# Low parts of every second weight block made by an adding transfer, in a decoder layer

## The chip, the cores and the metric

The kernel runs on one core of a Trainium2 chip. The time is in device microseconds (us) of one execution of the whole program. Engines are named as the profile names them: PE (TensorE matmul), PEld (its weight loads), DVE (VectorE), ACT (ScalarE), POOL (GpSimd), SP (SyncE, which only issues transfers here).

## The reference

One layer of a hybrid decoder, float32 in and out, 512 tokens of width 1024, 256 memory tokens:

```
x = x + 0.5 * swiglu(rms_norm(x), ffn1_gate, ffn1_up, ffn1_down)      # width 2816
z = rms_norm(x) @ w_in                                                # 7 groups of 512 columns
x = x + concat(hgrn2(z...), short_conv(z...)) @ w_out
q = rms_norm(x) @ w_q_mem;  k, v = split(rms_norm(mem) @ w_kv_mem)    # 4 heads of 256
x = x + softmax(q k^T / 16) v @ w_o_mem
x = x + 0.5 * swiglu(rms_norm(x), ffn2_gate, ffn2_up, ffn2_down)
out = rms_norm(x)
```

Some 26 million weights of float32 are read once.

## The kernel before

**Three products for one.** PE multiplies in float32r, which keeps fewer bits than float32. So each operand is split into a high part (the value rounded to float32r) and a low part (the value minus the high part, rounded), and a product a b is made as a_hi b_hi + a_hi b_lo + a_lo b_hi: `mm3`, lines 118 to 120, or three written-out matmuls in the stages w_i, w_v and w2d.

**Weight blocks.** Weights come in 202 blocks (called units in the code) of 128 partitions by 1024 elements (896 for two thirds of w1d). `weight_steps` numbers them by `n`, from 0, in the order in which the program asks for them, and gives each three tiles: `raw` (as loaded), `whi` and `wlo`. `load` (L105) issues the transfer from the queue of SP; `split` makes the high part on ACT (L109, a copy that rounds) and the low part on DVE (L110, raw minus high part). The blocks by stage:

| blocks | stage | PE work of a block |
|---|---|---|
| 0 to 43 | w1: first FFN, gate and up | 24 matmuls of 512 columns |
| 44 to 67 | w1d: first FFN, down | 21 or 24 of 512 |
| 68 to 95 | w_in and w_i: mixer inputs | 24 of 512 |
| 96 to 103 | w_out: mixer output | 24 of 512 |
| 104 to 111 | w_k: keys of the memory | 24 of 256 |
| 112 to 119 | w_q: queries | 24 of 512 |
| 120 to 127 | w_v: values of the memory | 12 of 512 |
| 128 to 135 | w_o: attention output | 24 of 512 |
| 136 to 179 | w2: second FFN, gate and up | 24 of 512 |
| 180 to 201 | w2d: second FFN, down | 24 of 512 (the last three by tokens) |

**Buffers.** `raw`, `whi` and `wlo` have three buffers each (`wpool`), given out in turn. Inside the two FFN stages blocks with n % 4 == 3 take a fourth pair of `whi` and `wlo` from the FFN's own pool instead (`extra`). So a block's split can start when PE has finished with the block three before it, or four before it in the FFN; its raw buffer is loaded anew when the split of the block three before has been made.

**Order.** The program is written with tile pools; a scheduler fixes each engine's order when the program is built, and puts in the waits. Each engine then runs its own list in order. POOL has little to do: three slices of the first loads (L105 with `queue=nc.gpsimd`), the power -0.5 of each norm (L151, L527), and some of the last norm (L752, L759).

The first three blocks are loaded and split in slices together with x (`first_tile`).

## Time and profile before

| | |
|---|---|
| time, median of 2 runs | 1131.24 us (1131.12 to 1131.37) |
| the profiled execution | 1130.89 us, span 1129.1 us |
| PE busy | 1119.5 us |
| DVE busy | 572.8 us |
| ACT busy | 391.1 us |
| POOL busy | 18.0 us |
| granted clock of PE | 0.999 |
| read from HBM | 109.09 MB |

The profile is of one execution. Busy times are the sums of an engine's instructions. In a row of the timeline stand the start and the length in us, engine, line, operation, tiles (written <- read), and in brackets how long the engine idled before and what ended that. In a row of groups stand the count, the busy time in us and the mean of one in ns, and the idle time before them. In a row of waits stand who waited for whom, us in total, how many times, and the longest. Rows of transfers give the count, KB each and the median us from issue to landing. In a row by stretches stand the engines' busy times in the order PE, PEld, DVE, ACT, POOL, then the granted clock, the DMA engines' mean busy share and GB/s.

### The profile page before, as it was taken

The page shows a single profiled execution, that of the slowest core. Times are in us where ns is not written, and L with a number is a line of the kernel's source. Part 1 is how long each engine was busy: PE and PEld are TensorE (multiplying, and loading weights), DVE is VectorE, ACT ScalarE, POOL GpSimd, SP SyncE. Part 2 cuts the span into 40 slices and gives each one's busy share as a digit, 9 for nine tenths or more (in the row PEclk, how much of TensorE's full clock was granted, in tenths as well). Part 3 has the DMA queues.
Part 4 walks back from the last instruction along what each step waited for, and adds up shares of the span by engine and source line. Part 5 has one row for each costly group of instructions (what it writes and reads, how often), then busy time and mean ns, then how long its engine had stood idle before and what let it go on. Part 6 is the DMA issues. An engine that isn't in the chain of part 4 may idle for free. (4 is left out here: it accounts for less than half of the span.)

```text
span 1129.1 us, 12928 instructions
## 1 busy us (share of the span) xinstructions
PE 1119.5 (99%) x5232; PEld 937.8 (83%) x5232; DVE 572.8 (51%) x829; ACT 391.1 (35%) x542; POOL 18.0 (2%) x21
## 2 busy tenths in 40 slices
PE   9999999999999999999999999999999999999997
PEld 7888888888888888888889888888888888888886
DVE  7644444443333466885677556564544444432223
ACT  6422332222222344324455246342333222231123
POOL 0000000000000000000100000000000000000002
PEclk9999999999999999999999999999999999999999
DMA  6322332323333222222144323123232223323311
GB/s 227 129 99 98 102 94 94 96 87 98 103 96 100 75 96 82 85 75 87 63 131 134 121 82 131 57 94 123 92 103 94 94 94 98 107 93 99 106 57 75
DMA packets 33195, 112.02 MB, mean 99 GB/s; under 512 B 3968, under 2 KB 4736, under 8 KB 33136
## 3 DMA queue, kind: packets, MB, share of 16 engines
q1 hardware_dynamic: 30960, 108.02, 29.1%
q10 hardware_dynamic: 2016, 2.66, 0.7%
q8 instruction: 41, 0.67, 0.2%
q0 software_dynamic: 160, 0.52, 0.2%
q14 instruction: 18, 0.15, 0.0%
HBM read 109.09 MB, written 2.10 MB: 98 GB/s over the span
## 5 line engine op out<-in xcount | busy, mean ns | idle before, releaser
L109 ACT ACTIVATE whi<-raw 128x1024 fp32r<-128x1024 f32 (+4 forms) x208 | 213.0, 1027 | 624.4 <-PE ps_f L119 274.1
L110 DVE TENSOR_TENSOR wlo<-raw,whi 128x1024 fp32r<-128x1024 f32 (+4 forms) x208 | 245.4, 1182 | 190.9 <-ACT whi L109 190.6
L212 DVE TENSOR_TENSOR u_f<-ps_f,rsb_f 128x512 f32<-128x512 f32 x44 | 30.4, 690 | 125.5 <-PE ps_f L120 125.5
L209 DVE TENSOR_TENSOR t_f<-ps_f,rsb_f 128x512 f32<-128x512 f32 x44 | 30.4, 690 | 79.0 <-PE ps_f L120 79.0
L213 DVE TENSOR_TENSOR u_f<-u_f,t_f 128x512 f32<-128x512 f32 x44 | 30.3, 692 | 4.0
L210 ACT ACTIVATE t_f<-t_f 128x512 f32<-128x512 f32 x44 | 27.7, 630 | 1.6 <-DVE t_f L209 1.1
L118 PE MATMUL psk<-memh,whi 128*128 128x256 f32 x64 | 18.2, 285 | 0.0
L119 PE MATMUL psk<-meml,whi 128*128 128x256 f32 x64 | 18.1, 284 | 0.0
L120 PE MATMUL psk<-memh,wlo 128*128 128x256 f32 x64 | 18.1, 283 | 0.0
L120 PE MATMUL ps_f<-x_f10h,wlo 128*128 128x512 f32 x44 | 17.3, 392 | 0.6 <-DVE wlo L110 0.6
L118 PE MATMUL ps_f<-x_f11h,whi 128*128 128x512 f32 x44 | 17.3, 393 | 0.4 <-ACT whi L109 0.4
L119 PE MATMUL ps_f<-x_f12l,whi 128*128 128x512 f32 x44 | 17.3, 393 | 0.0
L118 PE MATMUL ps_f<-x_f20h,whi 128*128 128x512 f32 x44 | 17.2, 391 | 0.0
L118 PE MATMUL ps_f<-x_f21h,whi 128*128 128x512 f32 x44 | 17.2, 390 | 0.0
L118 PE MATMUL ps_f<-x_f12h,whi 128*128 128x512 f32 x44 | 17.2, 390 | 0.0
L120 PE MATMUL ps_f<-x_f20h,wlo 128*128 128x512 f32 x44 | 17.2, 390 | 0.0
L119 PE MATMUL ps_f<-x_f10l,whi 128*128 128x512 f32 x44 | 17.2, 390 | 0.0
L120 PE MATMUL ps_f<-x_f11h,wlo 128*128 128x512 f32 x44 | 17.2, 390 | 0.0
L120 PE MATMUL ps_f<-x_f12h,wlo 128*128 128x512 f32 x44 | 17.2, 390 | 0.0
L120 PE MATMUL ps_f<-x_f17h,wlo 128*128 128x512 f32 x44 | 17.2, 390 | 0.0
L120 PE MATMUL ps_f<-x_f27h,wlo 128*128 128x512 f32 x44 | 17.2, 390 | 0.0
L118 PE MATMUL ps_f<-x_f15h,whi 128*128 128x512 f32 x44 | 17.2, 390 | 0.0
(1021 smaller groups left out, 3054.8 us busy)
## 6 DMA issues: line engine op xcount, KB each, us to landing
raw<-in_w SPq DMA_DIRECT2D x85, 512.0 KB, 3.4
raw<-in_w_in SPq DMA_DIRECT2D x24, 512.0 KB, 3.4
raw<-in_w2d SPq DMA_DIRECT2D x22, 512.0 KB, 3.4
raw<-in_w1d SPq DMA_DIRECT2D x16, 448.0 KB, 3.3
raw<-in_w1d SPq DMA_DIRECT2D x8, 512.0 KB, 3.5
raw<-in_w_out SPq DMA_DIRECT2D x8, 512.0 KB, 3.5
raw<-in_w_k SPq DMA_DIRECT2D x8, 512.0 KB, 3.4
raw<-in_w_q SPq DMA_DIRECT2D x8, 512.0 KB, 3.5
```

Source lines behind the costliest of these rows:

```text
L109: nc.scalar.activation(hi[:, c], raw[:, c], AF.Copy)
L110: nc.vector.tensor_tensor(lo[:, c], raw[:, c], r32(hi[:, c]), ALU.subtract)
L118: nc.tensor.matmul(out, lhsT=wh, rhs=xh, start=first, stop=False)
L119: nc.tensor.matmul(out, lhsT=wh, rhs=xl, start=False, stop=False)
L120: nc.tensor.matmul(out, lhsT=wl, rhs=xh, start=False, stop=last)
L209: nc.vector.tensor_tensor(t, ps[0], bc, ALU.mult)
L210: nc.scalar.activation(t, t, AF.Silu)
L212: nc.vector.tensor_tensor(u, ps[1], bc, ALU.mult)
L213: nc.vector.tensor_tensor(u, u, t, ALU.mult)
```

## The change

From block 5 on, the low part of each odd block is made without DVE. ACT writes minus the rounded raw block into `wlo`, and a transfer on POOL's queue then adds the block, read once more from HBM, onto that. Even blocks, and blocks 0 to 3, are as before. Lines from 115 on stand five lines lower in the changed kernel; its subtraction for the other blocks is L115.

```
         def split(k0, k1):
             c = slice(k0 * b, k1 * b)
             nc.scalar.activation(hi[:, c], raw[:, c], AF.Copy)
-            nc.vector.tensor_tensor(lo[:, c], raw[:, c], r32(hi[:, c]), ALU.subtract)
+            if n % 2 and n > 3:
+
+                nc.scalar.activation(lo[:, c], raw[:, c], AF.Copy, scale=-1.0)
+                nc.gpsimd.dma_start(lo[:, c], src[:, c], accum_op=ALU.add)
+            else:
+                nc.vector.tensor_tensor(lo[:, c], raw[:, c], r32(hi[:, c]), ALU.subtract)
```

PE's order stays as it was, but for one matmul of the first norm. On ACT in the stage w_k, here from block 109 to 111 (`kh` is the high part of the finished keys, `rsb_xa` a norm's row; the last number of a name is the program's own), there stood before:

```order
L109 ACTIVATE whi109_4530<-raw109_4529 128x1024
L581 ACTIVATE kh_3944<-km2_4450 128x256
L109 ACTIVATE whi110_4565<-raw110_4564 128x1024
L581 ACTIVATE kh_3944<-km3_4485 128x256
L170 ACTIVATE rsb_xa_4492<-psb_xa_4489 128x512
L109 ACTIVATE whi111_4600<-raw111_4599 128x1024
L581 ACTIVATE kh_3944<-km4_4525 128x256
```

and there stand now:

```order
L109 ACTIVATE whi109_4582<-raw109_4581 128x1024
L112 ACTIVATE wlo109_4583<-raw109_4581 128x1024
L586 ACTIVATE kh_3990<-km2_4501 128x256
L109 ACTIVATE whi110_4618<-raw110_4617 128x1024
L586 ACTIVATE kh_3990<-km3_4537 128x256
L175 ACTIVATE rsb_xa_4544<-psb_xa_4541 128x512
L109 ACTIVATE whi111_4653<-raw111_4652 128x1024
L586 ACTIVATE kh_3990<-km4_4577 128x256
L112 ACTIVATE wlo111_4654<-raw111_4652 128x1024
```

The negatives (L112) have come in: block 109's right behind its high part, block 111's with a key's high part between. Block 107's stands like block 111's, with `kh` of `km0` between. On ACT in the stage w_v (blocks 123 to 127) there stood only the high parts, one behind the other; now:

```order
L112 ACTIVATE wlo123_5273<-raw123_5271 128x1024
L109 ACTIVATE whi123_5272<-raw123_5271 128x1024
L109 ACTIVATE whi124_5291<-raw124_5290 128x1024
L112 ACTIVATE wlo125_5310<-raw125_5308 128x1024
L109 ACTIVATE whi125_5309<-raw125_5308 128x1024
L109 ACTIVATE whi126_5328<-raw126_5327 128x1024
L112 ACTIVATE wlo127_5347<-raw127_5345 128x1024
L109 ACTIVATE whi127_5346<-raw127_5345 128x1024
```

Here, and through w2d, the negative goes ahead of the high part of its block. In w_out the negative of block 101 stands behind its high part and six other operations (`x_xa2h` and `sq_xa` belong to the next norm of x, `memh` and `sq_mem` to the memory):

```order
L109 ACTIVATE whi101_4244<-raw101_4243 128x1024
L129 ACTIVATE x_xa2h_4133<-xall_102,vec_97 128x512
L140 ACTIVATE sq_xa_4137<-xall_102 128x512
L140 ACTIVATE sq_mem_4144<-mem4_4140 128x256
L129 ACTIVATE memh_3992<-mem6_4192,vec_97 128x256 x2
L140 ACTIVATE sq_mem_4149<-mem4_4140 128x256
L112 ACTIVATE wlo101_4245<-raw101_4243 128x1024
```

Before, nothing of block 101 stood on ACT after its high part.

On POOL, whose list held only the norms' powers between the opening and the end, the transfers (L113) now stand between them, here from w_out to w_k:

```order
L113 DMA wlo103_4339<-in_w_out 128x1024
L156 TENSOR_TENSOR rst_mem_4288<-rs_mem_4286,mhalf_77 128x2
L113 DMA wlo105_4419<-in_w_k 128x1024
L113 DMA wlo107_4507<-in_w_k 128x1024
L156 TENSOR_TENSOR rst_xa_4460<-rs_xa_4458,mhalf_77 128x4
L113 DMA wlo109_4583<-in_w_k 128x1024
```

Each transfer waits for the negative that ACT writes, and the power behind it in the list waits for its issue.

## The prediction

> **What bounds the kernel now.** I read the page first, then the waits of the matmul engine, then the weight split's own lines, then the times at which single blocks are made and used.

> ```profile
> PE 1119.5 (99%) x5232; PEld 937.8 (83%) x5232; DVE 572.8 (51%) x829; ACT 391.1 (35%) x542; POOL 18.0 (2%) x21
> ```
> ```profile
> PE warm L71 <- DVE mhalf L61: 1.1, 1, 1.1
> PE ps_f L120 <- DVE wlo L110: 0.6, 1, 0.6
> PE ps_f L118 <- ACT whi L109: 0.4, 1, 0.4
> PE psw L118 <- ACT yh1h L539: 0.3, 1, 0.3
> ```

> PE is busy for 1119.5 of 1129.1 us, and everything it waits for adds up to 2.4 us. So nothing that DVE, ACT or POOL stop doing can give back more than those few us: the change can only hide, or cost. The question is whether each low part is still there when PE's first L120 matmul asks for it.

> ```profile
> L110 DVE TENSOR_TENSOR wlo<-raw,whi 128x1024 fp32r<-128x1024 f32 x183 | 223.7, 1223 | 144.2 <-ACT whi L109 144.1
> L109 ACT ACTIVATE whi<-raw 128x1024 fp32r<-128x1024 f32 x183 | 193.9, 1061 | 567.9 <-PE ps_f L119 268.2 <-PE pso L730 74.4 <-issue 68.5
> ```

> A full block costs ACT 1.06 us (high part) and DVE 1.22 us (low part). ACT's waits are for PE: it starts block n as soon as PE has let go of the buffers of block n-3 (n-4 in the FFN stages, where a fourth pair exists). What matters is therefore the time from that start to PE's first use of the low part. In the first FFN, block 33:

> ```profile
> 173.23 1.06 ACT L109 ACTIVATE whi<-raw 128x1024 fp32r<-128x1024 f32 x1 [3.84 <-PE ps_f L119]
> ```
> ```profile
> 189.98 0.39 PE L120 MATMUL ps_f<-x_f10h,wlo 128*128 128x512 f32 x1
> ```

> 16.75 us lie between. The same distance recurs through both FFN products, which hold most of the blocks.

> **The change, part by part.** 99 blocks (odd, from 5 to 201) lose the DVE subtraction: 99 x 1.22 = 121 us of an engine that PE does not wait for; worth nothing. They gain an ACT copy with scale -1, priced as the L109 copy of the same shape: 99 x 1.06 = 105 us on an engine at 35%, hidden in the long stretches by ACT's own 567.9 us of waiting. And they gain a transfer that POOL issues after that copy. The new chain for an odd block is: buffer free, high part and negative copy on ACT (in either order), POOL's issue, landing. Call the last two L.

> No accumulating transfer stands in the trace. The nearest rows are the plain loads (KB each, us from issue to landing):

> ```profile
> q1 hardware_dynamic: 30960, 108.02, 29.1%
> ...
> raw<-in_w SPq DMA_DIRECT2D x85, 512.0 KB, 3.4
> ...
> raw<-in_w POOLq DMA_DIRECT2D x1, 320.0 KB, 7.1
> ...
> raw<-in_w SPq DMA_DIRECT2D x1, 64.0 KB, 3.1
> raw<-in_w POOLq DMA_DIRECT2D x1, 64.0 KB, 4.9
> raw<-in_w ACTq DMA_DIRECT2D x1, 64.0 KB, 3.3
> ```

> A 512 KB load from SP lands in 3.4 us. POOL's 64 KB took 4.9 us where SP's and ACT's took 3.1 and 3.3: 1.7 us more for the queue. Queue 1 held 16 engines for 29.1% of 1129.1 us, 328.6 us for 108.02 MB, or 1.6 us for 0.524 MB; an addition must fetch the destination too, so I count this stream once more. **L = 3.4 + 1.7 + 1.6 = 6.7 us**, an estimate. Its lower end is the plain load, 3.4. Its upper end takes POOL's opening rows, where all queues were loaded: (7.1 - 4.9) / 256 KB = 8.6 ns per KB, so 4.9 + 448 x 8.6 ns = 8.8 for 512 KB, and 3.9 for the second stream: 12.6. I take 6.7 because most of the loads meet emptier queues than the opening.

> In the FFN, two ACT operations (0.96 us from start to start, 1.06 for the last) leave 16.75 - 2.02 = 14.7 us for L: hidden up to 12.6. The tight places are where a block's matmuls are short. First w_k (blocks 104 to 111, 256 columns), odd blocks 107, 109 and 111; ACT rows, then PE's first use of each low part:

> ```profile
> 601.57 1.06 ACT L109 ACTIVATE whi<-raw 128x1024 fp32r<-128x1024 f32 x1 [0.77 <-PE psk L119]
> 602.53 0.40 ACT L581 ACTIVATE kh<-km 128x256 fp32r<-128x256 f32 x1
> ...
> 608.26 1.06 ACT L109 ACTIVATE whi<-raw 128x1024 fp32r<-128x1024 f32 x1 [2.40 <-issue]
> ...
> 614.47 1.06 ACT L109 ACTIVATE whi<-raw 128x1024 fp32r<-128x1024 f32 x1 [1.48 <-PE psk L119]
> 615.43 0.40 ACT L581 ACTIVATE kh<-km 128x256 fp32r<-128x256 f32 x1
> ```
> ```profile
> 608.37 0.28 PE L120 MATMUL psk<-memh,wlo 128*128 128x256 f32 x1
> ...
> 614.58 0.28 PE L120 MATMUL psk<-memh,wlo 128*128 128x256 f32 x1
> ...
> 620.34 0.28 PE L120 MATMUL psk<-memh,wlo 128*128 128x256 f32 x1
> ```

> For 107 and 111 a kh copy stands between the high part and the negative. The negative ends at 602.53 + 0.40 + 1.06 = 603.99, at 608.26 + 0.96 + 1.06 = 610.28 and at 615.43 + 0.40 + 1.06 = 616.89, which leaves 4.38, 4.30 and 3.45 us. A stall moves everything behind it, but a block's buffer comes from three blocks back. So 107 stalls by L - 4.38; 109, whose buffer came free before that stall, only by the 0.08 that is left; 111, freed by block 108, moved with the first stall and stalls by L - 3.53. Together 2L - 7.83 = **5.6 us**.

> w_v (blocks 120 to 127, 12 matmuls each) puts the negative first. Blocks 123 and 127:

> ```profile
> 682.77 1.06 ACT L109 ACTIVATE whi<-raw 128x1024 fp32r<-128x1024 f32 x1 [0.36 <-PE psvm L645]
> ...
> 693.65 1.06 ACT L109 ACTIVATE whi<-raw 128x1024 fp32r<-128x1024 f32 x1 [1.66 <-PE psvm L645]
> ```
> ```profile
> 688.24 0.39 PE L644 MATMUL psvm<-wlo,memh 128*128 128x512 f32 x1
> ```
> ```profile
> 699.12 0.39 PE L644 MATMUL psvm<-wlo,memh 128*128 128x512 f32 x1
> ```

> 688.24 - 683.83 = 4.41 for 123, and the same for 127; 125 between them is covered by the first stall. 2 x (L - 4.41) = **4.6 us**. Three single blocks remain: 101 in w_out, whose negative now stands behind the last sq_mem; the last block, 201; and 131 in w_o, as an example of the next tightest.

> ```profile
> 575.40 0.40 ACT L135 ACTIVATE sq_mem<-mem 128x256 f32<-128x256 f32 x1
> ```
> ```profile
> 582.05 0.39 PE L120 MATMUL psw<-yc0h,wlo 128*128 128x512 f32 x1
> ```
> ```profile
> 1100.27 1.06 ACT L109 ACTIVATE whi<-raw 128x1024 fp32r<-128x1024 f32 x1 [4.38 <-PE pso L730]
> ```
> ```profile
> 1107.09 0.39 PE L729 MATMUL pso<-wlo,a_f221h 128*128 128x512 f32 x1
> ```
> ```profile
> 719.67 1.06 ACT L109 ACTIVATE whi<-raw 128x1024 fp32r<-128x1024 f32 x1 [4.62 <-PE pswo L119]
> ```
> ```profile
> 731.03 0.39 PE L120 MATMUL pswo<-at0h,wlo 128*128 128x512 f32 x1
> ```

> 101: 582.05 - (575.40 + 0.40 + 1.06) = 5.19, a stall of **1.5 us**. 201 (negative first): 1107.09 - 1101.33 = 5.76, a stall of **0.9 us** right before the end. 131: 731.03 - 721.69 = 9.34, hidden. Sum: 6L - 27.6 = 12.6 us, 1.1%.

> The rest costs nothing. The negative waits, as DVE's subtraction did, for PE's last low-part matmul of the buffer's former block; behind it on ACT stand the next high part and, in the FFN, the silu and the split of the product, and each is 1.06 us later at most, which the margin of 14.7 covers. On POOL the transfers share a queue with the six power operations of the norms; the closest is rst_xa, between the transfers of 107 and 109:

> ```profile
> 605.68 1.01 POOL L151 TENSOR_TENSOR rst_xa<-rs_xa,mhalf 128x4 f32<-128x4 f32 x1 [15.81 <-ACT whi L109]
> ```

> It runs after 107's negative (603.99) and is done before 109's (610.28). SP's reload of an odd block's raw buffer now waits for ACT's negative instead of DVE; raw blocks land well ahead. The engines' load in w_k, where a new transfer every 5.8 us meets two loads:

> ```profile
> 598.00:622.00 24.00, 24.00 (x199) 23.84 (x198) 17.45 (x29) 12.62 (x19) 1.01 (x1) 1.00 0.46 152
> ```

> A share of 0.46, with 3.2 us more per 5.8 us, comes to about full. That is why I do not go below 6.7 here.

> **The profiled execution** took 1130.89 us (span 1129.1), 0.35 below the median of 1131.24. 1130.89 + 12.6 = **1143.5 us**.

> **The rivals.** (a) *Hidden anyway, not slower than before.* If POOL's issue costs little and the addition nothing, L is near 4.4 and the sum is about 1 us (only 111): 1132. For it: the 3.4 us row. Against it: the 4.9 us row. It decides below L = 4.6. [...]

> (b) *The addition is slow: slower by over 2%.* If the engines add at half the pace at which they fetch the two streams (3.2 us more, L = 9.9), or the queues in w_k are full, L passes 8.4, where 6L - 27.6 is 22.6 us, 2% of 1131. At L = 10 the six tight stalls cost 32.4, and of the ten blocks with a margin like 131's (in w_in, w_q and w_o), whose stalls cover each other in pairs, five pay 0.7 each: 1167. At 12.6: 48.0 + 5 x 3.3, 1195. For it: no row shows an addition, and the opening's rows are slow. Against it: the FFN would still hide all of it.

> (c) *DVE holds up the issue.* If a transfer's issue waits for a DVE operation, it loses at most one of L110's 1.22 us: L = 7.9, sum 19.9, 1151. [...]

> (d) *It doesn't do what it says:* if the transfer wrote instead of adding, L would be 5.1 and the sum 3.8 us, 1135; inside the range.

> **How the numbers follow.** Forecast (L from 4.6 to 8.4, with (d)): 0.45. (a) 0.14. (b) 0.35, of which a third beyond L = 10.5. (c) 0.04. Faster by over 2%: PE's 1119.5 us forbid it, 0.02 for what I don't see. 2% is about what a measurement of this kernel tells from no change. So within 2%: 0.45 + 0.14 + 0.04 = 0.63; slower 0.35. The range runs from 1133 (half of (a) left out) to 1172 (L near 10.5).

> **What would show it.** The page: DVE down to about 450, ACT up to about 496, 99 rows of L113 transfers with about 6.7 us to landing. PE's waits: psk, psvm, psw and pso on wlo transfers of 2 to 3 us each, none for ps_f. If ps_f waits, L is over 14.7 and the time is far beyond my range. If PE waits at whi, ACT's added copies are late, which I costed at nothing. If L is right and the stalls are not at these blocks, my reading of the buffers is wrong.

## The result, and the profile after

| kernel | median us | profiled execution us | span us |
|---|---|---|---|
| before | 1131.24 | 1130.89 | 1129.1 |
| changed | 1160.91 (1159.06 and 1162.77) | 1159.06 | 1157.3 |

The ratio is 1.0264, 95% interval 1.0246 to 1.0282: slower by 29.7 us, where 12.6 were forecast. Between the two profiled executions lie 28.2 us.

The first part of the page (busy us and share of the span), and two of its queue lines (packets, MB, share of the 16 DMA engines' span):

```profile
PE 1126.5 (97%) x5232; PEld 940.7 (81%) x5232; DVE 463.2 (40%) x730; ACT 478.4 (41%) x641; POOL 104.1 (9%) x120
...
q1 hardware_dynamic: 30960, 108.02, 29.7%
q0 software_dynamic: 14416, 51.91, 25.0%
```

DVE fell to 463 us and the transfers stand on queue 0, as the change says. PE has the same 5232 matmuls, but is "busy" 7.0 us longer than in the 1119.5 us before: some matmuls became slower, not only later. PE's waits for transfers (us in total, times, longest):

```profile
PE psk L125 <- DMA wlo<-in_w_k: 5.9, 4, 2.1
PE psvm L649 <- DMA wlo<-in_w_v: 5.5, 2, 3.0
PE ps_f L125 <- DMA wlo<-in_w: 3.2, 1, 3.2
PE psw L125 <- DMA wlo<-in_w_out: 2.9, 1, 2.9
```

Eight waits for transfers, 17.5 us. By PE's rows they stand at blocks 101 (2.87), 105 (1.52), 107 (0.18), 109 (2.11), 111 (2.08), 123 (2.48), 127 (3.05) and 137 (3.17). Block 111, which the prediction worked out, now reads so; ACT's negative, then PE's first use of the low part:

```profile
624.13 1.04 ACT L112 ACTIVATE wlo<-raw 128x1024 fp32r<-128x1024 f32 x1
...
633.34 0.39 PE L125 MATMUL psk<-memh,wlo 128*128 128x256 f32 x1 [2.08 <-DMA wlo<-in_w_k]
```

From the negative's end (625.17) to the use lie 8.2 us. By stages, from POOL's issue to landing, beside SP's plain load of w_k (KB each, median us):

```profile
wlo<-in_w POOLq DMA_DIRECT2D x42, 512.0 KB, 7.5
...
wlo<-in_w2d POOLq DMA_DIRECT2D x11, 512.0 KB, 6.9
raw<-in_w_k SPq DMA_DIRECT2D x8, 512.0 KB, 4.1
...
wlo<-in_w_k POOLq DMA_DIRECT2D x4, 512.0 KB, 7.3
```

POOL issues 0.30 us after the negative's end; that comes on top.

Two more losses are not waits. The first is the clock granted to PE. Two pairs of neighbouring windows of 3.41 us, around the waits at 111 and at 123 (behind the five engines' times stands the granted clock; 1.00 is full):

```profile
630.77:634.18 3.41, 1.33 (x12) 1.13 (x11) 0.85 (x2) 2.31 (x3) 0.59 (x1) 1.00 0.59 175
634.18:637.60 3.42, 3.42 (x19) 3.42 (x18) 0.00 (x0) 0.00 (x0) 0.27 (x1) 0.50 0.87 199
...
702.45:705.86 3.41, 0.93 (x5) 0.47 (x4) 0.00 (x0) 2.00 (x2) 0.85 (x1) 1.00 1.03 324
705.86:709.28 3.42, 3.42 (x10) 2.65 (x9) 0.00 (x0) 0.00 (x0) 0.00 (x0) 0.50 1.05 259
```

PE was idle for 2.08 and 2.48 us in the first window of each pair, and ran the second one at half clock (1.00, then 0.50). There are three such windows, at 586.40, 634.18 and 705.86, behind the waits at 101, 111 and 123. PE had idled for 2.70 us in the window before the first of them (582.99 to 586.40). Each is recorded as 3.413 us long, and from the first to the second lie 14 times 3.413 us and to the third another 21 times: all three stand on one grid of such windows. In the first and the third a matmul of 512 columns started every 0.427 us, where 0.227 was usual in w_out and w_v. By the granted 0.50 each did the work of 1.7 us in 3.41, so they lost about 5.1 us together, as an estimate. Before the change there was no such window until PE had ended.

The second loss is at the end: POOL's last long operation of the program is a drain (three drains; shortest, median and longest in ns). Before and after:

```profile
L843 POOLq DRAIN  x3: 34/102/901, 1123.9 to 1128.7; - x3
```
```profile
L848 POOLq DRAIN  x3: 46/102/6782, 1149.7 to 1157.0; - x3
```

The long one takes 6.8 us in place of 0.9 and is over at 1156.48; SP's first drain, behind the outputs, stands at 1154.0 already. From PE's last matmul to the end of the span go 9.5 us in place of 7.1: 2.4 us.

**The account of the 28.2 us:** 17.5 of waits, 5.1 of half clock, 2.4 at the end, 1.3 at two small shifts (0.67 at block 4, 0.61 where PE waits for `yh1h`), and 1.4 behind the five waits that no half window follows (PE is 0.25 to 0.29 us later behind 105, 107, 109, 127 and 137 than the wait alone explains). 0.5 is left over. What makes the two small shifts, and the slower pace behind the five waits, is open.

### The profile page after: what moved, and what is told of

Its sections match the earlier page's. It is cut to its first block, busy times and chain, and to the rows that moved or that the text cites. A ratio compares the mean times of both kernels' runs of the same rounds, so it can differ in the third digit from the quotient of the medians.

```text
span 1157.3 us, 13129 instructions
## 1 busy us (share of the span) xinstructions
PE 1126.5 (97%) x5232; PEld 940.7 (81%) x5232; DVE 463.2 (40%) x730; ACT 478.4 (41%) x641; POOL 104.1 (9%) x120
## 3 DMA queue, kind: packets, MB, share of 16 engines
q1 hardware_dynamic: 30960, 108.02, 29.7%
## 5 line engine op out<-in xcount | busy, mean ns | idle before, releaser
L109 ACT ACTIVATE whi<-raw 128x1024 fp32r<-128x1024 f32 (+4 forms) x208 | 212.7, 1026 | 551.1 <-issue 226.3
L115 DVE TENSOR_TENSOR wlo<-raw,whi 128x1024 fp32r<-128x1024 f32 (+4 forms) x109 | 125.4, 1155 | 189.9 <-ACT whi L109 189.6
L112 ACT ACTIVATE wlo<-raw 128x1024 fp32r<-128x1024 f32 (+1 forms) x99 | 102.7, 1037 | 46.5 <-PE pso L734 37.3
L113 POOL DMA_DIRECT2D wlo<-in_w x42 | 36.0, 856 | 415.3 <-ACT wlo L112 415.3
L196 DVE SCALAR_TENSOR_TENSOR xall<-psd_f,xall 128x512 f32<-128x512 f32 x8 | 5.5, 692 | 41.7 <-PE psd_f L125 41.7
L113 POOL DMA_DIRECT2D wlo<-in_w_in x12 | 10.3, 857 | 128.9 <-ACT wlo L112 100.2
L113 POOL DMA_DIRECT2D wlo<-in_w1d x12 | 10.2, 852 | 111.3 <-ACT wlo L112 111.3
L113 POOL DMA_DIRECT2D wlo<-in_w2d x11 | 9.4, 853 | 112.9 <-ACT wlo L112 112.9
L649 PE MATMUL psvm<-wlo,memh 128*128 128x512 f32 x32 | 13.2, 412 | 5.5 <-DMA wlo<-in_w_v 5.5
L125 PEld LDWEIGHTS psk<-memh,wlo 128*128 128x128 f32 x64 | 12.9, 202 | 6.7 <-DMA wlo<-in_w_k 6.7
## 6 DMA issues: line engine op xcount, KB each, us to landing
raw<-in_w SPq DMA_DIRECT2D x85, 512.0 KB, 4.0
wlo<-in_w POOLq DMA_DIRECT2D x42, 512.0 KB, 7.5
raw<-in_w_in SPq DMA_DIRECT2D x24, 512.0 KB, 4.0
raw<-in_w2d SPq DMA_DIRECT2D x22, 512.0 KB, 4.2
wlo<-in_w_in POOLq DMA_DIRECT2D x12, 512.0 KB, 7.7
wlo<-in_w2d POOLq DMA_DIRECT2D x11, 512.0 KB, 6.9
raw<-in_w1d SPq DMA_DIRECT2D x8, 512.0 KB, 3.7
```

The source lines that it names most:

```text
L109: nc.scalar.activation(hi[:, c], raw[:, c], AF.Copy)
L112: nc.scalar.activation(lo[:, c], raw[:, c], AF.Copy, scale=-1.0)
L113: nc.gpsimd.dma_start(lo[:, c], src[:, c], accum_op=ALU.add)
L115: nc.vector.tensor_tensor(lo[:, c], raw[:, c], r32(hi[:, c]), ALU.subtract)
L125: nc.tensor.matmul(out, lhsT=wl, rhs=xh, start=False, stop=last)
L649: nc.tensor.matmul(p, lhsT=a[:, c], rhs=wl[:, j], start=False, stop=False)
```

## The experiments

The theory (T): the loss is made where PE waits for a transfer in eight blocks, by the half-clock windows that those waits set off, and by POOL's drain. The rival (R): the added traffic, or ACT's second copy, slows the whole kernel.

### Only the loose blocks, only the tight blocks

```
-            if n % 2 and n > 3:
+            if n % 2 and n > 3 and n not in (99, 101, 105, 107, 109, 111, 123, 125, 127, 137, 201):   # e1
+            if n in (99, 101, 105, 107, 109, 111, 123, 125, 127, 137, 201):                           # e2
```

> 88 of the 99 transfers stay; the odd blocks whose low part has less than about 8 us between its negative and PE's use (99, 101, 105, 107, 109, 111, 123, 125, 127, 137, 201) are subtracted on DVE again. Theory T (the loss is PE waiting in eight of these blocks, 17.5 us, the half-clock windows behind three of those waits, 5.1 us, and 2.4 us at the end until POOL's drain is done): no PE wait for a transfer, no new half-clock window, only the drain and about 1 us of small shifts are left, 1133 to 1136 us. Rival R (the transfers' traffic or ACT's second copy slows the whole kernel, each transfer about alike): 88/99 of 29.7 us, about 1157 us.

> Only the 11 odd blocks with a short way from negative to use (99, 101, 105, 107, 109, 111, 123, 125, 127, 137, 201) take the transfer, the other 88 are subtracted on DVE. T: the same eight waits, 17.5 us, and two to four half-clock windows of 1.7 us; if POOL's drain grows with the number of transfers before it, the end costs nothing here: 1152 to 1157 us. R: 11/99 of 29.7 us, 1134.5 us.

With the 88 loose transfers the ratio is 1.0041 (1.0025 to 1.0056; median 1136.2, from 1133.41 to 1139.04); with the 11 tight ones 1.0267 (1.0228 to 1.0306; median 1160.46). Eleven transfers cost what ninety-nine do, 3.5 us more than T had asked for at most. PE's waits with the 11:

```profile
PE psk L125 <- DMA wlo<-in_w_k: 7.3, 4, 3.1
PE psvm L649 <- DMA wlo<-in_w_v: 5.5, 2, 2.9
PE psw L125 <- DMA wlo<-in_w_out: 3.8, 2, 2.3
PE ps_f L125 <- DMA wlo<-in_w: 2.4, 1, 2.4
```

19.0 us where T had 17.5, and five half-clock windows where it had two to four: block 99 waits too (1.53 us). With the 88, one new wait is left, at block 113, which came next:

```profile
PE psq L125 <- DMA wlo<-in_w_q: 0.7, 1, 0.7
```

No half window, and 2.5 us more than before in the profiled execution, which is the fastest of this kernel; the median is 0.2 us over T's range. What its other executions lost beyond that has no trace. Their granted clock is on record: 0.995 and 0.996 in the three longest, 0.998 in the other four. 0.002 to 0.003 of some 1138 us is 2.3 to 3.4 us, about one or two half-clock windows as an estimate; what set them off stays open. R, as a loss that each transfer causes alike, is out: it asked for 1157 and 1134.5.

### The two late negatives

```
-                nc.scalar.activation(lo[:, c], raw[:, c], AF.Copy, scale=-1.0)
+                if n in (101, 137):
+                    nc.vector.tensor_scalar(lo[:, c], raw[:, c], -1.0, None, op0=ALU.mult)
+                else:
+                    nc.scalar.activation(lo[:, c], raw[:, c], AF.Copy, scale=-1.0)
```

> As the changed kernel, but the negatives of blocks 101 and 137 are made on DVE, so they no longer stand behind the x and memory copies in ACT's list. T: the waits at 101 (2.87 us) and 137 (3.17 us) go, and the half-clock window behind 101 (1.7 us); 105, covered less by 101's stall, keeps 1.5 us: 1151 to 1155 us. Rival (these two are late because their transfers are slow, not because their negatives start late): 1158 us or more.

1154.41 (ratio 1.0206, 1.0191 to 1.0221), as T forecast, and 6.5 us less than with all negatives on ACT. Why 137 was late shows in ACT's timeline of the changed kernel; its high part, and behind seven copies of the next stage its negative:

```profile
774.63 1.06 ACT L109 ACTIVATE whi<-raw 128x1024 fp32r<-128x1024 f32 x1 [3.79 <-PE pswo L124]
775.60 0.71 ACT L129 ACTIVATE x_f20h<-xall,vec 128x512 fp32r<-128x512 f32 x1
...
779.80 0.71 ACT L129 ACTIVATE x_f26h<-xall,vec 128x512 fp32r<-128x512 f32 x1
780.42 1.04 ACT L112 ACTIVATE wlo<-raw 128x1024 fp32r<-128x1024 f32 x1
```

With the negatives on DVE, 137 no longer waits, 101 waits 0.47 us, and the half window behind 101 is gone; 99, whose transfer took 8.5 us here and 6.6 in the changed kernel, now waits 1.70. The waits' sum fell to 14.3 us. The order in ACT's list is a cause of its own.

### A fourth low buffer

```
-                  wpool.tile([P, 1024], F32R, tag=t, name=f"{t}{n}") for t in ("whi", "wlo"))
+                  wpool.tile([P, 1024], F32R, tag=t, name=f"{t}{n}", bufs=3 + (t == "wlo"))
+                  for t in ("whi", "wlo"))
# e5 beside it: raw with bufs=2. e9, e10 beside it: the tags sq and t1 of tmp with bufs=1
# e5, e9: the changed kernel. e10: the kernel before the change
```

> All 99 accumulating transfers stay, but the low parts have 4 buffers and the raw blocks 2, so a negative can start one block earlier in the stages with three buffers (all but the FFN's odd blocks). T: the landing stays at about 7 us, but 5.5 us or more of lead are added in w_k and w_v, and 137's negative goes ahead of the x_f2 copies: no wait of PE over 1 us there, no half-clock window; 1133 to 1138 us with the drain. R (traffic or ACT's copies, everywhere): unchanged, 1155 us or more. If two raw buffers are too few, PE waits for whi instead, which the trace would show.

1161.45 (1.0270, 1.0248 to 1.0292): T missed, and the time doesn't speak for R either, since the edit brought waits of its own. ACT in w_k, and PE's new wait in the opening:

```profile
621.09 1.06 ACT L113 ACTIVATE wlo<-raw 128x1024 fp32r<-128x1024 f32 x1 [4.21 <-DMA raw<-in_w_k]
```
```profile
PE psb_f L174 <- DVE dg_f L166: 6.5, 1, 6.5
```

With two raw buffers the negative waited for its raw block instead. So the test was made again with three.

> The run with four low buffers paid for them with a raw buffer, and then PE and ACT waited for raw loads. Here the fourth low buffer (and with it a negative that can start one block earlier) stands beside three raw buffers; the room comes from the second buffers of the squares (sq) and of the u/ob temporaries (t1). All 99 accumulating transfers stay. T: w_k, w_v, 101 and 137 get 5 us or more of lead, no PE wait for a transfer over 0.5 us, no half-clock window; with POOL's drain 2.4 us over the control kernel with the same buffers and no transfers: 1133 to 1138 us. R (the transfers' traffic or ACT's second copy slows these stages even where they come in time): 1150 us or more.

> Control for the run before: the kernel before the change with the same four low buffers and the single sq and t1 buffers, no transfers. PE bounds it: 1130.5 to 1134 us.

1147.6 (1.0144, 1.0128 to 1.0159), against the control's 1136.35 (1.0045, 1.0029 to 1.0062), which is over its forecast too: with its single buffers PE waits 4.2 us for a norm's sum of squares in the opening. The loss from the transfers is then 11.3 us instead of 29.7. More lead takes most of it away, but T had forecast that all but the drain's 2.4 us would go, and 1138 at most: a miss, between T and R. What PE still waits for:

```profile
PE psk L126 <- DMA wlo<-in_w_k: 3.7, 2, 2.0
...
PE psvm L650 <- DMA wlo<-in_w_v: 2.2, 2, 1.5
```

They are the waits at 107 and 111 and at 125 and 127, and behind 111 stands a half-clock window. In w_k 107's negative stands in ACT's list behind work of the end of w_out, and 111's waits again for its raw block. ACT's row, and SP's loads between 600 and 640 us (KB each, median us to landing):

```profile
622.20 1.06 ACT L113 ACTIVATE wlo<-raw 128x1024 fp32r<-128x1024 f32 x1 [1.04 <-DMA raw<-in_w_k]
```
```profile
raw<-in_w_k SPq DMA_DIRECT2D x4, 512.0 KB, 5.5
```

5.5 us, where 3.4 was usual before. To that extent R is right in one place: where the tight transfers lie close together, the loads that feed them land later too (4.1 us in the median in the changed kernel's w_k, 3.5 where the transfer does not add; see below).

### The low part used later

PE's order alone is changed in w_out, w_k, w_v and the first two blocks of the second FFN: all products of the high part, then those of the low part. For w_k:

```
-            for k in range(KT):
-                mm3(p[:, :MEM], wh[:, k], wl[:, k], memh[:, k], meml[:, k], k == 0, k == KT - 1)
+            high_first(p[:, :MEM], range(KT), wh, wl, lambda k: memh[:, k], lambda k: meml[:, k])
```

> As the changed kernel with all 99 transfers, but in w_out, w_k, w_v and the first two blocks of the second FFN PE multiplies all of a block's high part before its low part (the same matmuls in another order), so the low part is needed 14 matmuls later (6 in w_v): 3.1 to 3.3 us later in w_k, w_out and block 137, 1.3 us in w_v. T: the waits at 101, 105, 107, 109, 111 and 137 shrink to under 0.7 us each, 123 and 127 to 1.2 to 1.8 us each, and no window of the clock has 1.8 us of idle, so no half-clock window is left: 1136 to 1141 us, 2.4 us of it POOL's drain. R (traffic and copies slow these stages anyway, so later use moves nothing): 1150 us or more.

> Control: the kernel before the change with the same order of matmuls and no transfers. PE's work is the same and it hardly waited: 1130 to 1132.5 us by every theory.

With all 99 transfers 1141.69 (1.0092, 1.0074 to 1.0110), 0.7 over T's range and far from R's 1150; without them 1132.38 (1.0009, 0.9999 to 1.0019). 9.3 us are left of 29.7. PE's waits for transfers:

```profile
PE psk L132 <- DMA wlo<-in_w_k: 2.3, 3, 1.1
PE psvm L661 <- DMA wlo<-in_w_v: 2.3, 3, 1.2
```

4.6 us, no half window, and the drain's 2.4 us. 2.3 us are not accounted for. The transfers themselves were no faster (101: 7.6 us from the negative's end to landing, 111: 8.4; 7.5 and 8.1 in the changed kernel); only the place of the need moved. It is the fastest version with all the transfers, and still slower than the kernel before: PE bounds that one, and nothing waited for the DVE time that the change frees.

### The price of the addition

The same 99 transfers, but they overwrite the negative instead of adding to it, so the subtraction is left out:

```
-                nc.gpsimd.dma_start(lo[:, c], src[:, c], accum_op=ALU.add)
+                nc.gpsimd.dma_start(lo[:, c], src[:, c])
```

> All 99 transfers from POOL stay, behind the same negative, but overwrite instead of adding (the addition is left out: the low part is then the block itself). Theory A (the addition is what makes a packet of 4096 B take 328 ns where a plain one took 159, so about half of the excess of the landing over a plain load): landing about 5 to 5.5 us after the negative instead of 7.2, each wait about 2 us shorter, 101, 127 and 137 alone left with about 1 us each, no half-clock window behind them; with the drain 1135 to 1139 us. Theory B (POOL's queue is the price, with or without adding): landing stays at 7 us, and the time at 1155 us or more.

1143.38 (1.0103, 1.0088 to 1.0118). The queue's line and the landing in w_k of both kinds:

```profile
q0 software_dynamic: 14416, 51.91, 13.0%
...
raw<-in_w_k SPq DMA_DIRECT2D x8, 512.0 KB, 3.5
...
wlo<-in_w_k POOLq DMA_DIRECT2D x4, 512.0 KB, 4.5
```

So theory A holds for the landing: in w_k POOL's queue cost 1.0 us over SP's (3.5 to 4.5) and 0.3 ahead of it; the addition cost 2.8 (4.5 to 7.3). A packet of 4096 B took 174 ns here in the median and 328 ns with the addition. The time is 4 us over A's forecast. 101, 127 and 137 did not wait, as A had them do, but 125 in w_v took 7.4 us, made PE wait 2.65 us and set off the only half window, and w_k still waited 1.1 us. And the drain was longer than with the addition:

```profile
L848 POOLq DRAIN  x3: 46/93/8986, 1131.2 to 1140.7; - x3
```

From PE's last matmul to the end went 11.7 us, 2.2 more than A had counted.

### What sets off the half clock

The kernel before the change, with a small matmul ahead of each of 38 products that waits for a chain of DVE copies:

```
+            if name == "f2" and m > 2:
+                q = 2 * m + j - 6
+                d = tmp.tile([P, P], F32R, tag="t2", name=f"gap{q}")
+                nc.vector.tensor_copy(d, prev[0][:, :P])          # the bank of the product before
+                for i in range(q // 2):                           # e11: q // 2 % 6
+                    nc.vector.tensor_copy(d, r32(d))
+                nc.tensor.matmul(p[:, :P], lhsT=ones_r, rhs=d, start=True, stop=True)
```

> The kernel before the change, with a gap of PE ahead of each of the 38 products 3 to 21 of the second FFN: a small matmul that waits for a chain of 1 to 19 DVE copies which starts when the product before is done. The gaps grow from some 0.5 to some 4 us and fall anywhere on the 3.41 us grid. G1 (a window of the grid runs at half clock when PE was idle 1.8 to 1.9 us or more in the window before it, as in the five runs so far: 1.87 us and more did, 1.79 and less did not): the half windows follow exactly those windows, gaps up to 1.7 us never cost more than themselves, and gaps from 3.7 us on always cost 1.7 us more. G2 (only a window that is idle throughout does it): no half window for gaps under 3.4 us. G3 (a gap's own length decides): half windows behind every gap above one length, wherever it lies on the grid.

> The gaps of the run before it (e6) were mostly longer than a window. Here the chains have 1 to 6 copies, so gaps of some 0.5 to 3 us lie ahead of the 38 products. G1: behind every window of the 3.41 us grid with 1.87 us or more of idle comes one at half clock, behind none with 1.79 us or less that ran at full clock itself. G2 (only a window that is idle throughout): no half window at all, and a time that is longer by the gaps' sum alone. G3 (the gap's own length decides): gaps of 2 to 3 us all cost 1.7 us more, also where the grid splits them into 1.0 to 1.5 us on each side.

Of the first run's 38 gaps 31 were longer than a window, up to 7.8 us, which tells the theories apart in few places (1396.52 us in all); the second run (1289.41 us) decides. Two gaps of the same 2.39 us, each in the windows of the grid:

```profile
833.60:837.01 3.41, 2.73 (x12) 1.89 (x11) 0.64 (x2) 0.82 (x1) 0.00 (x0) 1.00 0.00 0
837.01:840.43 3.42, 1.71 (x8) 1.45 (x9) 1.65 (x4) 0.87 (x2) 0.00 (x0) 1.00 0.25 66
840.43:843.84 3.41, 3.41 (x17) 2.83 (x16) 0.00 (x0) 0.00 (x0) 0.00 (x0) 1.00 0.22 88
1065.71:1069.12 3.41, 1.02 (x5) 0.53 (x4) 2.29 (x5) 1.69 (x2) 0.00 (x0) 1.00 0.00 0
1069.12:1072.54 3.42, 3.42 (x9) 2.75 (x10) 0.00 (x0) 0.00 (x0) 0.00 (x0) 0.50 0.44 153
```

## Why the prediction was wrong

**What bounds the kernel** was read rightly: PE does, and 121 us less on DVE bought nothing. The mechanism was right too: the low part of a few tight blocks comes late.

**L**, the time from the negative's end to landing, was predicted as 6.7 us and came out at 7.5: 0.3 to the issue and 7.2 in the median from there to landing. At the eight blocks that waited it ran from 6.6 to 8.5. Its parts: plain load 3.4 (3.5 measured beside plain transfers), queue 1.7 (1.3 measured, with the 0.3), addition 1.6 (2.8 measured). The estimate for the addition took the DMA engines' time. That part was good: queue 0 went from 13.0% of 1141.0 us to 25.0% of 1157.3, 1.4 us more a transfer. But the landing grew by twice that. In the two blocks at the end that no raw load disturbed, it took 5.37 and 5.55 us with the addition and 3.75 and 3.62 without it, 1.8 more. In the seven kernels with adding transfers all 13 of them with no load beside them landed in 5.4 to 5.6 us. So the rest came where raw loads were under way at the same time.

**Rival (a)**, which needed L under 4.6 us, is out by the 7.5. Even the transfer without the addition took 4.5 us from issue to landing in w_k, and 3.62 and 3.75 where no load disturbed it; with the 0.3 to the issue w_k's come to 4.8, above 4.6 already.

**The stalls that were named**, by block: w_k 5.6 predicted, 5.9 measured; w_v 4.6 and 5.5; 101 1.5 and 2.87; 201 0.9 and none, because its transfer was one of the undisturbed ones. Together 12.6 and 14.3 us. In w_k the blocks were others: 105 already waited, for 1.52 us, which covered 107 and left 109 exposed. Before the change 6.81 us were left for L at 105 (its high part started at 592.90, PE's use at 601.73), 0.1 more than the predicted L, and its L was 8.5. That the sum hardly changed by this is luck in part.

**"The rest costs nothing" is the step that failed**, with a sum that priced a wait at its own length. Three terms stood at nothing.

(1) Block 137, 3.2 us. The prediction took a negative to stand right behind its high part in the FFN, with 14.7 us left for L, and did not look where ACT's list put it at the border between w_o and the second FFN, as it had done for 101. Before the change, the high part of 137 started and PE first used its low part at

```profile
752.31 1.06 ACT L109 ACTIVATE whi<-raw 128x1024 fp32r<-128x1024 f32 x1 [3.79 <-PE pswo L119]
```
```profile
763.67 0.39 PE L120 MATMUL ps_f<-x_f20h,wlo 128*128 128x512 f32 x1
```

so 9.3 us were left for L behind two operations, and the seven copies took 4.8 of these. That ps_f never waits fell with it, though L was far below 14.7.

(2) The half clock: three of the eight waits set off a half-clock window, 1.7 us each by the granted 0.50, 5.1 in all.

(3) The end of the program was taken as it was: POOL's drain, 2.4 us.

Beside these three, L was put 0.8 us too small, and the named stalls came out 1.7 us longer. Together that is 12.4 of the 15.6 us by which the profiled execution missed the forecast; the small shifts, the pace behind the waits and the remainder are the rest.

**The rivals.** (b), slower by over 2%, is where the time came out, but not by its mechanism: it needed L over 8.4, and L was 7.5 in the median. The range held the time only because (b) had drawn it up to 1172. (c) is out: POOL issued 0.30 us behind the negative's end at each of the eight blocks, with no wait for DVE. (d) is out: 4.5 us against 7.3 is the addition. All that the likeliest case left out has the same sign.

## What to carry to other kernels

PE bounds this kernel, and the price of its waits was not their length alone: 2.08 us of idle inside one window of 3.41 us (111) cost 3.8, and 2.11 us that fell into two windows, 0.81 and 1.30 (109), cost 2.4. Before work is moved to another engine's list, look at the borders of the stages, where the list mixes two of them, and at the end of the program, where queues are drained. Where an operand comes late, ask first whether its consumer has other work that can go ahead: the order of PE's matmuls alone took 20 of the 29.7 us away.

## What the runs showed of the hardware that was not expected

**The clock granted to PE.** It fell to 0.50 for whole windows of 3.413 us, three times in the changed kernel, and PE had idled for 2.70, 2.08 and 2.48 us in the window before (the waits at 101, 111 and 123). 127's wait of 3.05 us (1.25 and 1.79 in two neighbouring windows) and 137's of 3.17 (1.63 and 1.54) were longer, and the clock stayed at 1.00 behind both; in the run with the 11 transfers the same wait of 127, 2.94 us, had 2.25 in one window, and a half window followed. So in these runs a window that PE spent idle only in part, for 2.08 us of 3.41, was followed by half clock. What makes the clock change is not shown.

**POOL's drain** at the end was longer, the more adding transfers had gone through its queue: 0.9 us in the kernel before, where only the opening's three loads did, and

```profile
L848 POOLq DRAIN  x3: 46/93/1799, 1153.6 to 1158.4; - x3
```
```profile
L848 POOLq DRAIN  x3: 46/93/5882, 1124.9 to 1131.3; - x3
```

1.8 us with 11 more and 5.9 with 88 more, where 99 took 6.8. 4.4 us of it cost nothing in each of three runs (6.8 cost 2.4, 5.9 cost 1.5 and 9.0 cost 4.6 at the end). Why it took 9.0 us for 99 transfers without the addition is open.
